# Four m tiles of x on GpSimd's queue, in transfers of 15 partitions

## The chip, the cores and the metric

The kernel runs on one core of a Trainium2 chip. The metric is the device time of one execution in microseconds (us). A profile of one execution gives, beside that time, the span of its instructions and what each engine did: PE (TensorE), PEld (its weight loads), DVE (VectorE), ACT (ScalarE), POOL (GpSimd) and SP (SyncE, which here only issues transfers). Sixteen DMA engines move the data between HBM and the on-chip memory.

## The reference

```python
batch, m, k, n = 16, 512, 1024, 768
# x: (batch, m, k), weight: (k, n), sub_value: (batch, m, n), all float32
return (np.matmul(x, weight) - sub_value).astype(np.float32)
```

One weight serves all batches, so this is a single product of (8192 x 1024) by (1024 x 768), less a matrix of the size of the output.

## The kernel before, in words

The 8192 rows are 64 m tiles of 128 rows. `SEGMENTS` puts them in eight groups of 8: partition p of a group holds 8 consecutive rows, so that a transfer of n tiles of a group moves, for each partition, one contiguous row of n x 4 KB of x, or n x 3 KB of `sub_value` or of the output. "x 56" below is the transfer of x that begins with tile 56; s stands for `sub_value` and o for the output.

For each tile: SP loads x into `x_ring` (16 tiles deep) and s into `so_ring` (32 tiles deep). ACT casts x to float16 (`cast`, L330). x is then transposed, for most tiles by TensorE as pairs of halves read as float32 words (L348), after which ACT copies the result from PSUM (L361); for the nine pairs named in `ON_DVE` by DVE in blocks of 32 (L381). TensorE multiplies the transposed tile with the float16 weight that stays on chip, 16 matmuls into one of three product buffers `po_b` (L200). DVE subtracts s from the product into `so_ring` (`finish`, L430), and SP stores the output from there. TensorE's order is written by hand: the transposes of tile t stand between the matmuls of tile t - 2. The cast of tile t is put on ACT at the matmuls of tile t - 4 (t - 7 for a pair in `ON_DVE`), ahead of the copies of later transposes. Each engine runs its instructions in order.

SP's transfers run in the order of the list `TRANSFERS`, and each waits on SP, with all later ones behind it, until its ring places are free: x for the casts of the tiles 16 before, s for the landing of the outputs 32 before, o for the subtractions. Entries of kind "p" are x as well, but `issue` puts them on GpSimd's own queue (L260 to L269), where they wait apart from SP. In the kernel before there is one, tile 63, split by `PARTS` into partitions 120 to 125, 0 to 120 and 125 to 128. It waits for the cast of tile 47, which had the place before, and for the landing of tile 62. The cast of tile 63 waits for the semaphores of all three parts.

Of the kernel before, what the change touches and what calls it, by code (L numbers as in the profile page):

```python
# [14 lines left out]
NX, NSO = 16, 32  # L15
# [14 lines left out]
    ('x', 0, 1), ('w', 0, 1), ('x', 1, 1), ('w', 1, 1), ('x', 2, 1), ('w', 2, 1),  # L30
    ('x', 3, 2), ('w', 3, 1), ('s', 0, 1), ('x', 5, 3), ('s', 1, 3), ('x', 8, 4),
    ('s', 4, 4), ('x', 12, 4), ('s', 8, 8), ('x', 16, 2), ('x', 18, 6), ('s', 16, 8),
    ('x', 24, 8), ('o', 0, 8), ('s', 24, 8), ('x', 32, 8), ('s', 32, 8), ('x', 40, 8),
    ('o', 8, 8), ('o', 16, 8), ('s', 40, 8), ('x', 48, 8), ('s', 48, 8), ('x', 56, 7), ('p', 63, 1),
    ('o', 24, 8), ('o', 32, 8), ('s', 56, 8), ('o', 40, 8), ('o', 48, 8), ('o', 56, 5),
    ('o', 61, 2), ('o', 63, 1),
]

PARTS = (120, 125), (0, 120), (125, 128)


class Queue:
# [65 lines left out]
def kernel(  # L108
# [7 lines left out]
    nc = tc.nc  # L116

    x_flat = x.flatten_outer_dims()
# [4 lines left out]
    _, N = weight.shape  # L123
# [6 lines left out]
    def view(flat, at, n):  # L130

        first, size = next(one for one in SEGMENTS if one[0] <= at < sum(one))
        assert at + n <= first + size
        rows = flat[first * P : (first + size) * P].rearrange("(p j) c -> p j c", p=P, j=size)
        return rows[:, at - first : at - first + n]
# [6 lines left out]
    def sbuf(name, shape, dtype):  # L142
        return ctx.enter_context(nc.sbuf_tensor(name, shape, dtype)).ap()
# [10 lines left out]
    x_ring = sbuf("x_ring", [P, NX, K], F32)  # L154
# [12 lines left out]
    counter = {}  # L167
# [4 lines left out]
    def count(name):  # L172
        so_far[name] += 1
        return (counter[name], 1)

    sp, pe = Queue(nc, nc.sync), Queue(nc, nc.tensor)
    act, dve, pool = Queue(nc, nc.scalar), Queue(nc, nc.vector), Queue(nc, nc.gpsimd)
# [6 lines left out]
        out=along, data0=ones, data1=ones, initial=0.0, op0=mybir.AluOpType.mult, op1=mybir.AluOpType.add,  # L184
    ), waits=[(counter["ident"], 1)], then=count("ident"))
    dve.add(lambda: nc.vector.transpose(across, along), waits=[(counter["ident"], 3)], then=count("ident"))
    for a in range(P // Q):
        here = slice(a * Q, (a + 1) * Q)
        dve.add(lambda here=here: nc.vector.tensor_tensor(  # L189
            out=ident[here, here], in0=along[here], in1=across[here], op=mybir.AluOpType.is_equal,  # L190
# [16 lines left out]
    landed = {}  # L207
    cast_at, evac_at, pair_at, turn_at, mul_at, finish_at, w_at = {}, {}, {}, {}, {}, {}, {}
# [22 lines left out]
    def lane(tag):  # L231

        for one in lanes:
            if one["tags"] <= known:
                break
        else:
            one = {"sem": tc.alloc_semaphore(f"lane{len(lanes)}"), "value": 0, "tags": set()}
            lanes.append(one)
        one["value"] += 16
        one["tags"].add(tag)  # L240
        return one["sem"], one["value"]

    def issue():
        nonlocal known
        while todo:
            kind, at, n = todo[0]
            span = set(range(at, at + n))
            old = {t - NX if kind == "x" else t - NSO for t in span}
            need, by = {
                "w": (set(), "o"),  # L250
                "x": ({t for t in old if t >= 0}, "cast"),
                "p": ({at - NX}, "cast"),
                "s": ({t for t in old if t >= 0}, "o"),
                "o": (span, "finish"),
            }[kind]
            if not need <= done[by]:
                return
            todo.pop(0)
            done["x" if kind == "p" else kind] |= span
            if kind == "p":  # L260
                here, there = x_ring[:, at % NX], view(x_flat, at, 1)[:, 0]
                waits, landed["x", at] = [(counter["cast"], cast_at[at - NX]), *landed["x", at - 1]], []
                for low, high in PARTS:
                    sem = tc.alloc_semaphore(f"part{low}")
                    pool.add(lambda low=low, high=high, here=here, there=there: nc.gpsimd.dma_start(  # L265
                        out=here[low:high], in_=there[low:high], max_dma_last_dim=2048,
                    ), waits, (sem, 16))
                    landed["x", at].append((sem, 16))
                continue  # L269
            if kind == "w":  # L270

                first = NSO - 2 * (n_c - at)
                st = so_ring[:, first : first + 2]
                sem, value = lane((kind, at))
                sp.add(lambda st=st, at=at: nc.sync.dma_start(out=st, in_=w_c[at]), then=(sem, 16))  # L275
                for r in range(2):
                    dve.add(
                        lambda at=at, r=r, st=st: nc.vector.tensor_copy(out=w_sb[:, at, r], in_=st[:, r]),  # L278
                        waits=[(sem, value)], then=count("w"),
                    )  # L280
                    staged[first + r] = so_far["w"]
                w_at[at] = so_far["w"]
                continue
            ring, size, flat = {
                "x": (x_ring, NX, x_flat), "s": (so_ring, NSO, sub_flat), "o": (so_ring, NSO, out_flat)
            }[kind]
            here = ring[:, at % size : at % size + n]
            there = view(flat, at, n)
            waits = []
            if kind == "x" and need:  # L290
                waits.append((counter["cast"], max(cast_at[t] for t in need)))
                last = max(need, key=lambda t: cast_at[t])
                known |= {tag for t, tag in of_x.items() if t in cast_at and cast_at[t] <= cast_at[last]}
            if kind == "s":
                for t in need:
                    waits += landed["o", t]
                    known.add(of_o[t])
                for t in span:
                    if t % NSO in staged:
                        waits.append((counter["w"], staged.pop(t % NSO)))  # L300
                        known |= {("w", c) for c in w_at if w_at[c] <= waits[-1][1]}
            if kind == "o":
                waits.append((counter["finish"], max(finish_at[t] for t in need)))
                known |= {of_s[t] for t in finish_at if finish_at[t] <= max(finish_at[u] for u in need)}
            sem, value = lane((kind, at))
            for t in span:
                landed[kind, t] = [(sem, value)]
                {"x": of_x, "s": of_s, "o": of_o}[kind][t] = (kind, at)
            if kind == "o":
                here, there = there, here  # L310
            sp.add(lambda here=here, there=there: nc.sync.dma_start(out=here, in_=there), waits, (sem, 16))  # L311

    def cast(mi):
        assert mi in done["x"]
        done["cast"].add(mi)
        x_in = x_ring[:, mi % NX]
        first = mi - mi % 2
        waits = list(landed["x", mi])
        if first in ON_DVE:
            if mi == first:  # L320
                b, before = take("x16p", N16P, mi)
                if before is not None:
                    waits.append((counter["pair"], pair_at[before]))
            to = x16p_b[:, slot["x16p", first], mi - first]
        else:
            b, before = take("x16", N16, mi)
            if before is not None:
                waits.append((counter["turn"], turn_at[before]))
            to = x16_b[:, b]
        act.add(lambda: nc.scalar.copy(out=to, in_=x_in), waits, count("cast"))  # L330
        cast_at[mi] = so_far["cast"]
        issue()
# [92 lines left out]
    def finish(mi):  # L425
        assert mi in done["s"]
        done["finish"].add(mi)
        o = so_ring[:, mi % NSO].rearrange("p (h n) -> p h n", h=2)
        po = po_b[:, slot["po", mi]]
        dve.add(lambda: nc.vector.tensor_tensor(  # L430
            out=o, in0=po[:, :, :NS], in1=o, op=mybir.AluOpType.subtract
        ), [*landed["s", mi], (counter["mul"], mul_at[mi])], count("finish"))
        finish_at[mi] = so_far["finish"]
        issue()

    issue()


# [59 lines left out]
    for mi in range(HEAD + (EARLY is not None), n_mt):  # L498
# [3 lines left out]
        t = mi + TA  # L502
# [68 lines left out]
```

## Time and profile before

| | |
|---|---|
| median of 2 runs | 210.94 us (210.79 to 211.09) |
| the profiled execution: its time, its span | 210.47 us, 208.6 us |
| PE busy | 195.2 us, 94% |
| DVE busy | 128.1 us, 61% |
| ACT busy | 109.0 us, 52% |
| POOL busy | 3.0 us, 1% |
| DMA | 87.08 MB, 417 GB/s over the span |
| last output's transfer, 384 KB | 4.8 us from issue to landing |

The time of an execution is its span and some 1.9 us around it. Busy times are those of one execution; "to landing" is counted from the issue of a transfer to its completion semaphore. The views of the profile are the page (busy times, 40 equal slices of the span, DMA queues, the chain that ended last, groups of instructions by line, DMA issues), the waits, the timeline, and windows of time. In the page, q1 is SP's queue and q0 GpSimd's.

### The profile page before, as it was taken

What the parts mean: (1) busy time and instruction counts of PE and PEld (TensorE: products, weight loads), DVE (VectorE), ACT (ScalarE), POOL (GpSimd) and SP (SyncE); (2) the same over time, 40 slices, a digit from 0 to 9 for tenths busy, and PEclk for the clock granted to TensorE, in tenths of its full rate; (3) what the DMA queues carried; (4) which work ended last, traced back from release to release, by engine and by line L of the source; (5) the groups of instructions that cost most, each with busy time, mean ns of one, the idle gap of its engine ahead of it and who ended that gap; (6) DMA issues with size and microseconds to landing.
All of it is one profiled execution on the core that took longest, in us unless ns stands there. A gap on an engine that the chain in (4) does not pass through costs nothing.

```text
span 208.6 us, 2617 instructions
## 1 busy us (share of the span) xinstructions
PE 195.2 (94%) x1234; PEld 75.4 (36%) x700; DVE 128.1 (61%) x224; ACT 109.0 (52%) x113; POOL 3.0 (1%) x10
## 2 busy tenths in 40 slices
PE   6899699969999999999999999999999999999960
PEld 0233244324434433443443443344344344344310
DVE  2233224975993895597399389469739938942330
ACT  2655659506573761854745676183574746516300
POOL 1000000000000000000000000000000300000000
PEclk9999999999999999999999999999999999999997
DMA  6999999999999999999999999999999999999993
GB/s 204 421 428 429 437 423 431 449 435 427 424 440 446 371 443 433 444 421 411 455 440 427 415 429 448 430 452 404 424 441 428 433 432 423 443 424 433 421 418 155
DMA packets 5685, 87.08 MB, mean 417 GB/s; under 512 B 689, under 2 KB 689, under 8 KB 2097
## 3 DMA queue, kind: packets, MB, share of 16 engines
q1 hardware_dynamic: 5472, 86.51, 97.3%
q0 software_dynamic: 208, 0.52, 0.6%
q14 instruction: 4, 0.02, 0.0%
q8 instruction: 1, 0.02, 0.0%
HBM read 61.87 MB, written 25.17 MB: 417 GB/s over the span
## 4 chain that ended last, share of the span: by engine, by line
PE 75%; DMA 13%; DVE 6%; SPq 3%; issue 1%; DVEq 0%
PE po_b L200 67%; DMA so_ring<-in_sub_value_dram 13%; PE pt_b L348 8%; DVE xtp_b L381 3%; DVE so_ring L430 2%; SPq L311 2%; SPq L275 1%; SPq L566 0%; DVEq L61 0%; SPq L140 0%
## 5 line engine op out<-in xcount | busy, mean ns | idle before, releaser
L200 PE MATMUL po_b<-w_sb,xt_b 128*128 128x384 f16 x704 | 126.0, 326 | 0.9 <-DVE w_sb L278 0.8
L430 DVE TENSOR_TENSOR so_ring<-po_b,so_ring 128x768 f32<-128x768 f32 x64 | 60.7, 957 | 58.9 <-PE po_b L200 39.8
L361 ACT COPY xt_b<-pt_b 128x1024 f16<-128x1024 f16 x44 | 44.5, 1012 | 64.7 <-PE pt_b L348 63.8
L381 DVE STREAM_TRANSPOSE xtp_b<-x16p_b 32x256 f32<-32x256 f32 x144 | 62.7, 435 | 2.3
L200 PE MATMUL po_b<-w_sb,xtp_b 128*128 128x384 f16 x320 | 61.3, 326 | 1.8 <-DVE xtp_b L381 1.7
L410 PEld LDWEIGHTS <-xt_b 128*128 128x128 f16 x352 | 34.4, 98 | 58.4 <-issue 55.2
L330 ACT CAST x_b<-x_ring 128x1024 f16<-128x1024 f32 x46 | 47.2, 1048 | 5.5 <-DMA x_ring<-in_x_dram 5.5
L348 PE MATMUL pt_b<-ident,x_b 128*128 128x128 f32 x184 | 47.6, 274 | 1.9 <-ACT x_b L330 1.9
L348 PEld LDWEIGHTS pt_b<-ident,x_b 128*128 128x128 f32 x184 | 25.3, 141 | 45.0 <-issue 36.3
L330 ACT CAST x16p_b<-x_ring 128x1024 f16<-128x1024 f32 x18 | 18.8, 1046 | 14.8 <-DMA x_ring<-in_x_dram 14.8
L410 PEld LDWEIGHTS <-xtp_b 128*128 128x128 f16 x160 | 15.7, 98 | 20.3 <-issue 18.3
L278 DVE CAST w_sb<-so_ring 128x768 f16<-128x768 f32 x8 | 4.1, 557 | 12.0 <-DMA so_ring<-in_weight_dram 12.0
L200 PE MATMUL po_b<-idle_x,idle_w 128*128 128x512 f16 x26 | 7.7, 443 | 1.7 <-POOL idle_x L180 1.7
L265 POOL DMA_DIRECT2D x_ring<-in_x_dram x3 | 2.0, 668 | 136.7 <-DMA x_ring<-in_x_dram 136.7
L361 ACT COPY xtp_b<-pt_b 128x1024 f16<-128x1024 f16 x2 | 2.0, 1012 | 2.4 <-PE pt_b L348 2.4
L330 ACT ACT_TABLE_LOAD x1 | 1.3, 1283 | 0.9 <-SPq L140 0.9
L440 PEld LDWEIGHTS <-idle_w 128*128 128x128 f16 x4 | 0.4, 100 | 1.7 <-POOL idle_x L180 1.7
L189 DVE TENSOR_TENSOR ident<-along,across 32x32 f32<-32x32 f32 x4 | 0.7, 183 | 0.1
L181 DVE MEMSET ones<- 128x32 f32 x1 | 0.1, 85 | 1.0 <-SPq L140 1.0
L180 POOL MEMSET idle_x<- 128x512 f16 x1 | 0.5, 531 | 0.0
L489 POOL MEMSET mark<- 128x1 f32 x1 | 0.1, 99 | 24.0 <-ACT xtp_b L361 24.0
L512 ACT CAST stub<-ident 128x1 f16<-128x1 f32 x2 | 0.4, 194 | 0.0
(8 smaller groups left out, 1.2 us busy)
## 6 DMA issues: line engine op xcount, KB each, us to landing
so_ring<-in_sub_value_dram SPq DMA_DIRECT2D x7, 3072.0 KB, 24.2
out_dram<-so_ring SPq DMA_DIRECT2D x7, 3072.0 KB, 26.6
x_ring<-in_x_dram SPq DMA_DIRECT2D x4, 4096.0 KB, 21.6
x_ring<-in_x_dram SPq DMA_DIRECT2D x2, 2048.0 KB, 27.2
x_ring<-in_x_dram SPq DMA_DIRECT2D x1, 3584.0 KB, 21.9
so_ring<-in_weight_dram SPq DMA_DIRECT2D x4, 768.0 KB, 8.8
x_ring<-in_x_dram SPq DMA_DIRECT2D x1, 3072.0 KB, 28.3
x_ring<-in_x_dram SPq DMA_DIRECT2D x2, 1024.0 KB, 24.8
```

What stands on the lines that cost most here:

```text
L189: dve.add(lambda here=here: nc.vector.tensor_tensor(out=ident[here, here], in0=along[here], in1=across[here], op=mybir.AluOpType.is_equal, ...
L200: return nc.tensor.add_instruction(mybir.InstMatmult(name=nc.get_next_instruction_name(), engine=full.engine, ins=list(full.ins), outs=lis ...
L265: pool.add(lambda low=low, high=high, here=here, there=there: nc.gpsimd.dma_start(out=here[low:high], in_=there[low:high], max_dma_last_di ...
L275: sp.add(lambda st=st, at=at: nc.sync.dma_start(out=st, in_=w_c[at]), then=(sem, 16))
L278: lambda at=at, r=r, st=st: nc.vector.tensor_copy(out=w_sb[:, at, r], in_=st[:, r]),
L311: sp.add(lambda here=here, there=there: nc.sync.dma_start(out=here, in_=there), waits, (sem, 16))
L330: act.add(lambda: nc.scalar.copy(out=to, in_=x_in), waits, count("cast"))
L348: pe.add(lambda: nc.tensor.transpose(words, from_, ident), waits, count("turn") if last else None)
L361: act.add(lambda: nc.scalar.copy(out=to, in_=pt_b[:, b]), waits, count("evac"))
L381: dve.add(lambda: nc.vector.transpose(xt[b * Q : (b + 1) * Q, :, a * Q : (a + 1) * Q], x16[a * Q : (a + 1) * Q, :, b * Q : (b + 1) * Q],), ...
L410: pe.add(lambda weights=weights: nc.tensor.ldweights(weights, tile_position=(0, 0)), [w for w in waits if w[0] in ready])
L430: dve.add(lambda: nc.vector.tensor_tensor(out=o, in0=po[:, :, :NS], in1=o, op=mybir.AluOpType.subtract), [*landed["s", mi], (counter["mul" ...
```

## The change

Tiles 38, 39 and 62 leave SP's queue: the transfer x 32 has 6 tiles instead of 8, and x 56 has 6 instead of 7. They and tile 63 are loaded by GpSimd as two groups of two tiles. Each tile of a group goes in eight transfers of 15 partitions, first the eight of the one tile, then those of the other, and at the end one transfer of the last 8 partitions for each: 18 transfers to a group, each with a semaphore of its own. The group of tile 38 waits for the casts of tiles 22 and 23 alone; that of tile 62 for the casts of tiles 46 and 47 and for the landing of tile 61. Each of the four casts waits for the nine semaphores of its tile. No other instruction changes its place on any engine.

```diff
-    ('x', 24, 8), ('o', 0, 8), ('s', 24, 8), ('x', 32, 8), ('s', 32, 8), ('x', 40, 8),
-    ('o', 8, 8), ('o', 16, 8), ('s', 40, 8), ('x', 48, 8), ('s', 48, 8), ('x', 56, 7), ('p', 63, 1),
+    ('x', 24, 8), ('o', 0, 8), ('s', 24, 8), ('x', 32, 6), ('p', 38, 2), ('s', 32, 8), ('x', 40, 8),
+    ('o', 8, 8), ('o', 16, 8), ('s', 40, 8), ('x', 48, 8), ('s', 48, 8), ('x', 56, 6), ('p', 62, 2),
...
-PARTS = (120, 125), (0, 120), (125, 128)
+PARTS = [(j, low, low + 15) for j in range(2) for low in range(0, 120, 15)] + [(j, 120, 128) for j in range(2)]
...
             if kind == "p":
-                here, there = x_ring[:, at % NX], view(x_flat, at, 1)[:, 0]
-                waits, landed["x", at] = [(counter["cast"], cast_at[at - NX]), *landed["x", at - 1]], []
-                for low, high in PARTS:
-                    sem = tc.alloc_semaphore(f"part{low}")
-                    pool.add(lambda low=low, high=high, here=here, there=there: nc.gpsimd.dma_start(
-                        out=here[low:high], in_=there[low:high], max_dma_last_dim=2048,
+                here, there = x_ring[:, at % NX : at % NX + n], view(x_flat, at, n)
+                waits = [(counter["cast"], max(cast_at[t] for t in old))]
+                if at > NSO + 8:
+                    waits += landed["x", at - 1]
+                for t in span:
+                    landed["x", t] = []
+                for k, (j, low, high) in enumerate(PARTS):
+                    sem = tc.alloc_semaphore(f"part{at}_{k}")
+                    pool.add(lambda j=j, low=low, high=high, here=here, there=there: nc.gpsimd.dma_start(
+                        out=here[low:high, j], in_=there[low:high, j], max_dma_last_dim=2048,
                     ), waits, (sem, 16))
-                    landed["x", at].append((sem, 16))
+                    landed["x", at + j].append((sem, 16))
                 continue
```

## The prediction

> **What bounds the kernel now.** I read the page from the top: the busy table, the 40 slices, the DMA queues, then the chain, the waits, and the timeline of the last 50 us. The slices come first.
>
> ```profile
> PE   6899699969999999999999999999999999999960
> ...
> POOL 1000000000000000000000000000000300000000
> ...
> DMA  6999999999999999999999999999999999999993
> ...
> q1 hardware_dynamic: 5472, 86.51, 97.3%
> q0 software_dynamic: 208, 0.52, 0.6%
> ```
>
> TensorE and the 16 DMA engines are both full from the fourth slice or so to the end: two bounds side by side, so a delay in either is paid unless the other's buffers cover it. POOL shows one mark, in slice 32: the three transfers of tile 63. The line of q0 carries most of this forecast. Those three transfers have only 128 partition rows of 4 KB (0.52 MB), yet 208 packets, which is 16 x 13. The trace's records of single packets say what the 13 of each engine are: one packet per partition row, or an 8 byte stand-in on an engine that a transfer leaves out, and one 4 byte completion packet per transfer. Most engines have 2 + 9 + 2 packets for the three transfers (8 rows, or stand-ins, and a completion in the middle one).
>
> The DMA groups give the landing of these transfers, the timeline their issue and what consumes x at the end:
>
> ```profile
> x_ring<-in_x_dram POOLq DMA_DIRECT2D x1, 480.0 KB, 14.7
> ...
> x_ring<-in_x_dram POOLq DMA_DIRECT2D x1, 20.0 KB, 6.8
> x_ring<-in_x_dram POOLq DMA_DIRECT2D x1, 12.0 KB, 15.8
> ```
> ```profile
> 162.45 2.00 POOL L265 DMA_DIRECT2D x_ring<-in_x_dram  x3 [136.72 <-DMA x_ring<-in_x_dram]
> ```
> ```profile
> 187.26 1.01 ACT L361 COPY xt_b<-pt_b 128x1024 f16<-128x1024 f16 x1 [5.24 <-PE pt_b L348]
> 188.17 1.05 ACT L330 CAST x_b<-x_ring 128x1024 f16<-128x1024 f32 x1
> 189.12 0.19 ACT L512 CAST stub<-ident 128x1 f16<-128x1 f32 x1
> 190.29 1.01 ACT L361 COPY xt_b<-pt_b 128x1024 f16<-128x1024 f16 x1 [0.98 <-PE pt_b L348]
> 191.20 1.05 ACT L330 CAST x_b<-x_ring 128x1024 f16<-128x1024 f32 x1
> ```
> ```profile
> 190.69 0.27 PE L348 MATMUL pt_b<-ident,x_b 128*128 128x128 f32 x1
> ```
>
> A 12 KB transfer took 15.8 us: not its bytes cost, but its place in line. The two casts are tiles 62 and 63. The cast of 62 ends at 189.2 and TensorE's first transpose of tile 62 starts at 190.69, so 62 may be about 1.4 us late, that is, land by 189.5, before TensorE stops. Behind it on TensorE stand three transposes of 62, the rest of tile 60, and tiles 61 to 63. Nothing there can pass.
>
> **The turn of a software packet.** On every engine the packet records show strict alternation while both queues have work: one q0 packet, one q1 packet. A 24 KB row of q1 takes 0.91 us, a 4 KB row of q0 0.16, a stand-in or completion 0.01; one in nine q1 packets is itself a completion. So a q0 packet of any size waits 0.91 x 8/9 = 0.81 us on average. Tile 63: 12 waits of 0.81 and 8 rows of 0.16 make 11.0 us; the records span 167.2 to 177.7 on a typical engine, 10.5.
>
> [...]
>
> **The change, part by part.** Removed: the three transfers of tile 63, and from SP's queue tiles 38 and 39 (x 32 has 6 tiles instead of 8) and tile 62 (x 56 has 6 instead of 7). Added: two groups of 18 transfers on GpSimd. Each engine gets 16 rows per group, spread evenly, but also, per transfer, a completion, and a stand-in where it is left out. 16 transfers x 2 packets + 2 x 2 = 36 packets per engine and group, 20 of them carrying no data. Over both groups q0 should have 2 x 36 x 16 = 1152 packets.
>
> *Issue.* 18 x 0.668 us = 12 us per group on POOL, which has nothing else to do. It is hidden as long as one transfer takes under 2 turns, 1.8 us.
>
> *Tiles 38 and 39.* The wait is the cast of tile 23, which ends at 68.7 (timeline), no landing. First packets 4.6 us after the first issue, as at tile 63 (162.45 to 167.06): 73.4. 36 packets x 0.81 + 16 x 0.16 = 31.9, slightly more where rows are 32 KB (1.21 us): done by 107. Tile 38 is cast at 118.8. Margin over 10 us; cost nothing. SP's loads around it carry 2.4 us less and share with 2.5 us more: all later landings move by +0.3 us. The nearest deadline of those, s of tile 56 (landing 185.1, needed some 0.6 us later before TensorE misses a product buffer), holds, because x 56 is shorter by 8 x 0.15 = 1.2 us per engine and q0's rows beside it are about as many as before. One engine writes its output rows 3% slower than the others (0.945 against 0.912) and is the one that tile 63's 120 partitions left out; the even spread gives it 6 rows back, 0.9 us, which s 56 bears from that 1.2. From below: rows of x that leave SP's queue could bring s 56 1 us earlier; it is waited for by DVE alone, so no gain. I take 0.
>
> *Tiles 62 and 63.* x 56 lands at 161.85 - 1.2 + 0.3 = 161.0; issue at 161.6, first packets at 166.2. SP's queue has rows for all that time (outputs 32, s 56, outputs 40 and 48, 32 rows per engine). Tile 62 is complete with packet 34 (its last 8 partitions are the 17th transfer): 34 x 0.81 + 15 x 0.16 = 29.9, so 196.1; on the slow engine 24 output rows x 0.03 = 0.7 more: 196.8. Tile 63 comes with packet 36, 1.8 us later, in time for its own cast behind that of 62. The cast of 62 runs 196.8 to 197.9 instead of 188.17 to 189.22. TensorE, due at 190.69, goes on at 197.9: **stall 7.2 us**. ACT's copy of tile 61 waits behind this cast too, but is needed after it.
>
> *Clock.* 7.2 us idle is longer than the 4.4 us after which this trace shows the clock at 0.5. Coming back costs half of the ramp. The kernel's first matmuls start at 1.68 and the full clock is on record from 4.5: half of 2.8 is **1.4 us**. [...]
>
> *Tail.* Before, the last output was issued at about 202.5 and landed 4.8 us later, behind rows still queued. Delayed by 8.6 us it finds the queue nearly empty (outputs 48 end near 199): start of data after about 1.8 us, 1.0 us of rows (384 KB), 0.6 of spread, 3.4. **Gain 1.4 us**; bounds 0.8 and 2.
>
> *Waits.* Each of the four casts waits for 9 semaphores instead of 1 or 3; all but the last are long up. Under 0.5 us on ACT, hidden at 38 and 39, inside the rounding at 62.
>
> Sum: 7.2 + 1.4 - 1.4 = +7.2 us. The profiled execution took 210.47 (span 208.6 plus 1.9); 217.7 in that execution's terms. The median of the runs is 210.94, 0.47 above it: 218.1, and I say **218.0**.
>
> **Rivals.** (A) is the above, own range 214 to 222.5: landing 194.5 to 200.5 by how the turns fall, with or without the clock.
>
> (B) Not slower. Completions and stand-ins of many small transfers might be taken together with the row beside them, so that a transfer costs one turn: 18 turns x 0.81 + 2.5 = 17.1, tile 62 complete near 183, before 188.17. The point is 189.5: up to there nothing is lost. Then only packet overhead and the slow engine's 6 rows remain: 210.9 + 0.3 = 211.2. For it: when SP's queue gives only a completion in its turn, two q0 packets follow closely. Against: at tile 63 a completion sat behind a full 24 KB row on nearly every engine.
>
> (C) GpSimd becomes the limit. If one issue took 2.5 us instead of 0.67 (many transfers in flight, rings to refill), a group takes 45 us: tile 62 near 161.6 + 17 x 2.5 + 4 = 208, a stall of 18 us, and tile 38 at about 115, still in time: 210.9 + 18 + 1.4 - 1.4 = 229. Against: the three issues before took 572 to 754 ns.
>
> **How the numbers follow.** A 0.83, B 0.13, C 0.04. This measurement tells about 2% (4.2 us) from no change. Slower by more: A but for its lowest end, and C, 0.84; within: B and that end, 0.14; faster 0.02, within B, if even loading brings the last outputs forward further than I see. Range 212 to 223: A's with the upper part of B.
>
> **What would show it.** Right: q0 with 1152 packets; POOL busy twice for about 12 us, near 69 and 162; a new wait of ACT on x near 188 to 197, and of PE on ACT's cast, together most of the loss, with none near 119; granted clock 0.5 for a few us after; the last output landing in under 4 us. Wrong: x of tile 62 landing before 189 (then B), a stall near 119 or 187, or POOL busy far over 12 us per group (C).

## The result and the profile after

The changed kernel takes 227.55 us (median of 2 runs, 226.62 to 228.48) against 210.94: 1.079 times the time before, 95% interval 1.060 to 1.098. The forecast was slower, 218.0 with a range of 212 to 223. The direction was foreseen, and less than half of the loss: 7.1 of 16.6 us.

The page of the changed kernel, slices and DMA queues:

```profile
PE   7997899799999999989998999996999999703990
...
POOL 1000000000006910000000000000029500000000
PEclk9999999999999999999999999999999999975899
DMA  6999999999999999999999999999999999995372
GB/s 214 424 422 435 445 423 442 415 450 433 446 430 377 447 383 327 357 335 349 375 443 418 424 433 442 446 407 437 437 433 417 431 374 371 429 431 230 131 314 115
...
q1 hardware_dynamic: 5472, 84.94, 91.8%
q0 software_dynamic: 1152, 2.10, 2.6%
```

A slice is 5.62 us. The hole in PE near 200 us and the dip of the clock behind it are the ones that were forecast, and 1152 packets on q0 is the count that was forecast. What was not is in the row GB/s. In slices 16 to 20, 84 to 112 us, the DMA engines move 327 to 375 GB/s instead of some 430, while the row above it says that they are busy all the time. Slices 33 and 34 have it again. Busy engines that move less: their packets take longer.

The dip was forecast from these windows of the kernel before, where TensorE's work ends near 201.5 and half clock stands from 206 (third column from the end: the granted clock):

```profile
200.00:204.00 4.00, 1.48 (x10) 0.29 (x3) 0.96 (x1) 0.00 (x0) 0.00 (x0) 1.00 0.95 402
204.00:205.80 1.80, 0.00 (x0) 0.00 (x0) 0.00 (x0) 0.00 (x0) 0.00 (x0) 1.00 0.70 287
206.00:208.60 2.60, 0.00 (x0) 0.00 (x0) 0.00 (x0) 0.00 (x0) 0.00 (x0) 0.50 0.06 24
```

The timelines of the changed kernel, of GpSimd's transfers, of ACT's casts of tiles 62 and 63, and of TensorE's four transposes of tile 62 and the first of tile 63:

```profile
69.16 10.18 POOL L269 DMA_DIRECT2D x_ring<-in_x_dram  x18 [43.61 <-ACT x16p_b L334]
167.43 10.04 POOL L269 DMA_DIRECT2D x_ring<-in_x_dram  x18 [88.09 <-DMA x_ring<-in_x_dram]
```
```profile
204.75 1.04 ACT L334 CAST x_b<-x_ring 128x1024 f16<-128x1024 f32 x1 [11.81 <-DMA x_ring<-in_x_dram]
...
206.70 1.04 ACT L334 CAST x_b<-x_ring 128x1024 f16<-128x1024 f32 x1
```
```profile
205.85 0.47 PE L352 MATMUL pt_b<-ident,x_b 128*128 128x128 f32 x1 [8.75 <-ACT x_b L334]
...
207.39 0.42 PE L352 MATMUL pt_b<-ident,x_b 128*128 128x128 f32 x1
...
208.88 0.42 PE L352 MATMUL pt_b<-ident,x_b 128*128 128x128 f32 x1
...
210.27 0.27 PE L352 MATMUL pt_b<-ident,x_b 128*128 128x128 f32 x1
...
211.03 0.27 PE L352 MATMUL pt_b<-ident,x_b 128*128 128x128 f32 x1
```

The cast of tile 62 starts at 204.75 instead of 188.17, and TensorE stands for 8.75 us in front of the first transpose. The next ones are 1.5 us apart at first, at half clock, and 0.76 once the clock is back. But GpSimd's second group already starts 5 us later than before (167.43 against 162.45), so something was lost earlier.

TensorE runs the same 1234 matmuls in the same order in both kernels, so I subtracted the start of each from that of the same matmul before. The delay grows in a few steps:

| start before, us | delay after the step, us | what came late |
|---|---|---|
| up to 97 | 0.1 | |
| 97.2 | 1.3 | s of tile 24 |
| 120.7 to 121.4 | 2.8 | x 40 |
| 149.3 | 4.7 | s of tile 40 |
| 187.0 | 6.3 | s of tile 56 |
| 190.7 | 15.2 | x of tile 62 |
| to 192.8 | 17.3 | half clock |

For the first four steps the right column follows from the waits. The first fence is the kernel before, the second the changed one: DVE's subtractions of tiles 24, 40 and 56 and ACT's cast of tile 40.

```profile
89.60 0.96 DVE L430 TENSOR_TENSOR so_ring<-po_b,so_ring 128x768 f32<-128x768 f32 x1
...
136.85 0.96 DVE L430 TENSOR_TENSOR so_ring<-po_b,so_ring 128x768 f32<-128x768 f32 x1 [3.77 <-DMA so_ring<-in_sub_value_dram]
...
185.47 2.69 DVE L430 TENSOR_TENSOR so_ring<-po_b,so_ring 128x768 f32<-128x768 f32 x3 [2.67 <-DMA so_ring<-in_sub_value_dram]
...
115.01 1.05 ACT L330 CAST x16p_b<-x_ring 128x1024 f16<-128x1024 f32 x1 [2.48 <-DMA x_ring<-in_x_dram]
```
```profile
91.79 0.96 DVE L434 TENSOR_TENSOR so_ring<-po_b,so_ring 128x768 f32<-128x768 f32 x1 [2.08 <-DMA so_ring<-in_sub_value_dram]
...
142.82 1.82 DVE L434 TENSOR_TENSOR so_ring<-po_b,so_ring 128x768 f32<-128x768 f32 x2 [6.88 <-DMA so_ring<-in_sub_value_dram]
...
192.24 2.69 DVE L434 TENSOR_TENSOR so_ring<-po_b,so_ring 128x768 f32<-128x768 f32 x3 [4.76 <-DMA so_ring<-in_sub_value_dram]
...
121.05 1.05 ACT L334 CAST x16p_b<-x_ring 128x1024 f16<-128x1024 f32 x1 [7.26 <-DMA x_ring<-in_x_dram]
```

And TensorE's own waits in the changed kernel, at the first matmuls of tiles 28, 36, 46 and 59:

```profile
98.49 0.81 PE L200 MATMUL po_b<-w_sb,xtp_b 128*128 128x384 f16 x4 [0.97 <-DVE xtp_b L385]
...
123.14 0.81 PE L200 MATMUL po_b<-w_sb,xt_b 128*128 128x384 f16 x4 [1.06 <-ACT xt_b L365]
...
153.94 0.81 PE L200 MATMUL po_b<-w_sb,xtp_b 128*128 128x384 f16 x4 [1.72 <-DVE xtp_b L385]
...
193.25 0.81 PE L200 MATMUL po_b<-w_sb,xtp_b 128*128 128x384 f16 x4 [1.42 <-DVE so_ring L434]
```

The way from a late transfer to TensorE is indirect. DVE waits for s of tile 24, and the block transposes of tiles 28 and 29 stand behind that subtraction on DVE; s of tile 40 holds up those of tiles 46 and 47 in the same way. On ACT the cast of tile 40 waits for x 40, and the copy that TensorE needs for tile 36 stands behind it. s of tile 56 keeps the product buffers full. x 32 and x 48 came late too, but others ended the waits.

The span ends 16.2 us later (224.8 against 208.6). So 6.3 us are gone before tile 62 is even due. The forecast had nothing there.

The records of single packets say where. Of SP's 24 KB rows, those of outputs (stored rows) still take 0.92 us while GpSimd's packets stand between them (74 to 80 us); those of loads (loaded rows) take 1.14 us on average from 85 to 107 us, with a median of 1.20. Summed over the early group, loaded rows took 5.5 us per engine more than rows of their length take elsewhere (0.91 us for 24 KB, 1.06 for 28 KB, 1.21 for 32 KB). This is called the excess below.

### The profile page after: what moved, and what is told of

Read it like the earlier page. It is cut to its first block, busy times and chain, and to the rows that moved or that the text cites. A ratio compares the mean times of both kernels' runs of the same rounds, so it can differ in the third digit from the quotient of the medians.

```text
span 224.8 us, 2665 instructions
## 1 busy us (share of the span) xinstructions
PE 198.8 (88%) x1234; PEld 75.9 (34%) x700; DVE 127.9 (57%) x224; ACT 108.5 (48%) x113; POOL 21.2 (9%) x43
## 3 DMA queue, kind: packets, MB, share of 16 engines
q0 software_dynamic: 1152, 2.10, 2.6%
## 4 chain that ended last, share of the span: by engine, by line
DMA 60%; PE 24%; POOL 4%; ACT 4%; DVE 3%; issue 2%; SPq 1%; ACTq 0%; DVEq 0%
DMA x_ring<-in_x_dram 44%; PE po_b L200 21%; DMA so_ring<-in_sub_value_dram 16%; POOL x_ring L269 4%; PE pt_b L352 3%; ACT x_b L334 2%; DVE xtp_b L385 2%; ACT xt_b L365 1%; DVE so_ring L434 1%; SPq L315 1%; SPq L279 0%; ACTq L61 0%; SPq L61 0%; ACT x16p_b L334 0%; SPq L570 0%
## 5 line engine op out<-in xcount | busy, mean ns | idle before, releaser
L200 PE MATMUL po_b<-w_sb,xt_b 128*128 128x384 f16 x704 | 128.1, 329 | 1.9 <-ACT xt_b L365 1.1
L352 PE MATMUL pt_b<-ident,x_b 128*128 128x128 f32 x184 | 48.1, 276 | 10.4 <-ACT x_b L334 10.3
L269 POOL DMA_DIRECT2D x_ring<-in_x_dram x36 | 20.2, 564 | 131.7 <-DMA x_ring<-in_x_dram 88.1
```

The lines of the kernel that those rows point to most:

```text
L200: return nc.tensor.add_instruction(mybir.InstMatmult(name=nc.get_next_instruction_name(), engine=full.engine, ins=list(full.ins), outs=lis ...
L269: pool.add(lambda j=j, low=low, high=high, here=here, there=there: nc.gpsimd.dma_start(out=here[low:high, j], in_=there[low:high, j], max_ ...
L352: pe.add(lambda: nc.tensor.transpose(words, from_, ident), waits, count("turn") if last else None)
```

## The experiments

### Which group costs what

Tiles 62 and 63 alone in the new form; then tiles 38 and 39 alone. Diffs are against the changed kernel unless said otherwise, and "..." stands for lines left out.

```diff
-    ('x', 24, 8), ('o', 0, 8), ('s', 24, 8), ('x', 32, 6), ('p', 38, 2), ('s', 32, 8), ('x', 40, 8),
+    ('x', 24, 8), ('o', 0, 8), ('s', 24, 8), ('x', 32, 8), ('s', 32, 8), ('x', 40, 8),
```

> Tiles 62 and 63 go as in the changed kernel (18 transfers on GpSimd's queue), tiles 38 and 39 stay on SP's queue (x 32 with 8 tiles). Both theories on the slow load rows agree here; this run splits the loss by group. The forecast had all of the loss in this group: 218, with x of tile 62 cast at 196.8. From the changed kernel's trace, where from the first software packet to the cast of 62 some 33 us pass instead of the 30 of the forecast, and s of tile 56 is late as well: cast of 62 near 199 to 200, a stall of TensorE of about 9 to 10 us, the clock's return 2 us, a tail 1 us shorter: 220 to 222, and no delay of TensorE before 185 us.

Measured: 219.34 us, ratio 1.041 (1.039 to 1.043), a little under what was expected.

```diff
-    ('o', 8, 8), ('o', 16, 8), ('s', 40, 8), ('x', 48, 8), ('s', 48, 8), ('x', 56, 6), ('p', 62, 2),
+    ('o', 8, 8), ('o', 16, 8), ('s', 40, 8), ('x', 48, 8), ('s', 48, 8), ('x', 56, 7), ('p', 63, 1),
...
+PARTS_OF = {63: [(0, 120, 125), (0, 0, 120), (0, 125, 128)]}
...
-                for k, (j, low, high) in enumerate(PARTS):
+                for k, (j, low, high) in enumerate(PARTS_OF.get(at, PARTS)):
```

> Tiles 38 and 39 go as in the changed kernel, tiles 62 and 63 as in the kernel before (x 56 with 7 tiles, tile 63 in its three transfers). The forecast: +0.3 us, 211. From the changed kernel's trace: rows that SP's queue loads (24 KB) take 1.15 us on average instead of 0.91 while GpSimd's packets stand between them, stored rows stay at 0.91; x 40 and x 48 land late and TensorE is some 4.7 us behind at 150 us; nothing gives that back: 215 to 216.5.

Measured: 217.94 us, ratio 1.035 (1.032 to 1.039), above what was expected. The two losses, 8.6 and 7.2 us, come to 15.8 of the 16.6 of the whole change. The late group alone behaves nearly as forecast: TensorE has no delay until 187 us, then waits for the cast of tile 62, which starts at

```profile
198.76 1.04 ACT L334 CAST x_b<-x_ring 128x1024 f16<-128x1024 f32 x1 [10.90 <-DMA x_ring<-in_x_dram]
```

(ACT's timeline, late group alone) where the forecast had 196.8. The early group alone, which was put at 0.3 us, leaves TensorE 4.3 us behind at 149 us and 5.8 at 187; its excess is 5.6 us per engine. The rest of its 7.2 us lies behind TensorE's end and comes up again at the tail below.

### Completions, or rows?

The first guess came from the same packet records: a loaded row that was followed by one of GpSimd's completions was longer (1.24 us) than one followed by a data row (about 1.0). Two kernels have the same bytes under the same waits with fewer transfers.

```diff
-PARTS = [(j, low, low + 15) for j in range(2) for low in range(0, 120, 15)] + [(j, 120, 128) for j in range(2)]
+PARTS = [(j, 0, 128) for j in range(2)]
```

> Tiles 38, 39, 62 and 63 on GpSimd's queue under the same waits, but each in one transfer of 128 partitions: the same bytes, 2 transfers per group instead of 18. Completion theory (a loaded row of SP's queue that is followed by a completion of GpSimd's queue is held up by about 0.33 us, by a data row only 0.07): 18 packets per engine and group instead of 36, 2 completions: rows near 0.98, some 1.5 us of DMA time lost beside the loads in the early group, no stall on tile 62 (9 packets, complete near 176): 211 to 213. Data theory (any loaded row of GpSimd's queue beside a loaded row of SP's holds it up by about 0.25 us): 16 rows per engine still cost 4 us in the early group: 214 to 216, rows near 1.15.

Measured: 211.09 us, ratio 1.0018 (1.0011 to 1.0026). All of the loss is gone but 0.33 us.

```diff
+PARTS = [(j, low, low + 60) for j in range(2) for low in (0, 60)] + [(j, 120, 128) for j in range(2)]
```

> As the changed kernel, but with transfers of 60 partitions instead of 15 (4 rows per engine): 6 transfers per group, 28 packets at most per engine instead of 36. Completion theory: 6 x 0.33 + 16 x 0.07 = 3 us of DMA time lost beside loads in the early group, tile 62 complete near 188 to 190, a stall of 0 to 2 us: 212.5 to 215. Data theory: as with whole tiles 4 us and the stall: 215 to 217. In both, between whole tiles and transfers of 15.

Measured: 216.49 us, ratio 1.027 (1.025 to 1.029).

Transfers of 60 have an excess of 3.1 us per engine, just the 3 that the completion theory asked for, though the time lies above its range and within that of the data theory. Whole tiles speak against both. Their packets stand beside loads as well (129 of their data rows between 82 and 91 us, and completions), and the excess is 0.02 us, not 1.5. That refutes the data theory outright, and the completion theory too unless its cost depends on something else. With transfers of 60, moreover, it is the rows between two data rows that are slow (0.23 us over on average, from 80 to 101 us), with no completion next to them. What is left as a candidate is not what a packet is but which partitions its transfer takes, and with them perhaps which engine carries them.

### The same rows in two orders

Two kernels move tile 39 alone on GpSimd's queue, in 16 transfers of 8 partitions with a step of 4, in pairs of one from the lower half of the partitions (0, 4 .. 28) and one from the upper half (64, 68 .. 92); tile 63 goes as in the kernel before. They differ only in the order within each pair. That the order changes which engine carries which row was the author's guess; the records do not number the engines. First the lower half before the upper:

```diff
...
+PARTS = [(0, half + low, half + low + 29) for low in (0, 1, 2, 3, 32, 33, 34, 35) for half in (0, 64)]
...
+                        out=here[low:high:step, j], in_=there[low:high:step, j], max_dma_last_dim=2048,
...
```

> Only tile 39 leaves SP's queue (x 32 with 7 tiles), in 16 transfers of 8 partitions with a step of 4: 0, 4 .. 28 and 64, 68 .. 92 in turn, then the same from 1, 2, 3, 32, 33, 34 and 35; tile 63 goes as in the kernel before. Each engine gets 8 rows, 8 stand-ins and 16 completions, as many completions as in the early group of the changed kernel. [...] Completion theory: 16 x 0.33 = 5 us of lost DMA time beside loads, 214 to 216. Source theory (15 reads at once that lie 32 KB apart in HBM): no excess or more of it, the reads lie 128 KB apart here: 211 to 216.

Measured: 211.86 us, ratio 1.0053 (1.0033 to 1.0074), excess 0.04 us per engine. TensorE ends 0.16 us later than before; the rest of the 1.1 us lies behind its end (see the tail below).

The other order, against the run with the lower half first:

```diff
-PARTS = [(0, half + low, half + low + 29) for low in (0, 1, 2, 3, 32, 33, 34, 35) for half in (0, 64)]
+PARTS = [(0, half + low, half + low + 29) for low in (0, 1, 2, 3, 32, 33, 34, 35) for half in (64, 0)]
```

> [...]

Measured: 214.18 us, ratio 1.0205 (1.0141 to 1.0269), excess 2.5 us per engine. Its four runs, 213.8 to 216.7 us, all lie above the four with the lower half first, 211.4 to 212.1.

Windows of both, the run with the lower half first ahead: start and end, length, busy time of PE, PEld, DVE, ACT and POOL with instructions, granted clock, DMA share, GB/s.

```profile
88.00:95.00 7.00, 7.00 (x47) 2.80 (x26) 6.79 (x14) 3.90 (x5) 0.00 (x0) 1.00 0.99 425
95.00:102.00 7.00, 7.00 (x47) 2.70 (x25) 4.02 (x6) 2.71 (x4) 0.00 (x0) 1.00 0.97 414
```
```profile
88.00:95.00 7.00, 7.00 (x47) 2.77 (x26) 6.42 (x13) 3.90 (x5) 0.00 (x0) 1.00 1.03 399
95.00:102.00 7.00, 7.00 (x47) 2.75 (x26) 4.28 (x7) 2.69 (x4) 0.00 (x0) 1.00 1.00 371
```

The same number of transfers, packets, completions and bytes, the same engine shares (0.97 to 1.03), and 371 GB/s instead of 414 with nothing but the order changed. Loaded 24 KB rows take 0.912 us with the lower half first, 1.013 with the upper half first. The lower half first has 16 completions per engine, nearly as many as the changed kernel's group, and none of its excess: the completion theory falls here. In the reversed pair a loaded row behind a stand-in is as long as one behind a row of data (1.08 and 1.06 us on average, from 80 to 105 us; 0.95 behind a completion). So an engine is held up also where it carries no data of GpSimd's queue itself. That fits a row of another engine as the cause; no run shows which.

Two more runs, with the early group alone, test the rest. First, the source in HBM; the kernel then loads other rows of x for tiles 38 and 39, so its output is not the product and only its time counts:

```diff
...
-                        out=here[low:high, j], in_=there[low:high, j], max_dma_last_dim=2048,
+                        out=here[low:high, j], in_=x_flat[P * (at + j) + low : P * (at + j) + high] if at == 38 else there[low:high, j], max_dma_last_dim=2048,
...
```

> The early group of the changed kernel alone (tiles 62 and 63 as before), but its 15 rows come from 15 neighbouring rows of x in HBM, 60 KB in one piece, and not from rows 32 KB apart: the data of tiles 38 and 39 is other rows of x, all else is the same. Source theory: the excess of loaded rows goes (rows at 0.91, 211.2). [...]

Measured: 218.3 us, ratio 1.036 (1.034 to 1.037), excess 6.5 us per engine. That the rows lie 32 KB apart in HBM is not the cause. If the reversed pair changes which engine carries a row, it changes which one reads it from HBM as well as which one writes it, and no run separates the two; that rows from another place in HBM lose as much speaks for the side that is written.

Second, 16 partitions to a transfer:

```diff
...
+PARTS = [(j, low, low + 16) for j in range(2) for low in range(0, 128, 16)]
...
```

> The early group alone, in 16 transfers of 16 neighbouring partitions: 16 engines each, so no engine is left out and there are no stand-ins; 16 rows and 16 completions per engine, 32 packets. [...] Completion theory: 16 completions for 18, 216 to 218. If the stand-ins or the rotation of the left-out engine were the cause: 211.5.

Measured: 217.98 us, ratio 1.034 (1.032 to 1.036), excess 5.8 us per engine. In its profile the clock fell for 3.4 us as well, so the excess is the better measure here. Without stand-ins and without a left-out engine it is about that of the early group (5.6), so rotating the left-out engine is not what costs. The windows of transfers of 16 show 311 GB/s where whole tiles, below them, have 446:

```profile
88.00:95.00 7.00, 7.00 (x47) 2.66 (x25) 3.92 (x8) 3.91 (x4) 0.00 (x0) 1.00 0.94 311
```
```profile
88.00:95.00 7.00, 7.00 (x47) 2.70 (x25) 5.38 (x13) 3.90 (x5) 0.00 (x0) 1.00 1.04 446
```

### The turns of the late group, with little excess

The lower half first also allows a test of the step that was forecast: many packets, and little excess (0.5 us per engine, most of it in one burst near 180 us, against 1.4 in the late group alone). The late group alone, in 2 x 16 transfers of 8 partitions, each tile in 32 packets per engine (1024 packets on q0).

```diff
...
+PARTS = [(j, half + low, half + low + 29) for j in range(2) for low in (0, 1, 2, 3, 32, 33, 34, 35) for half in (0, 64)]
...
```

> [...] Turn theory (one packet of GpSimd's queue per packet of SP's): from a first packet near 165.9, 31 waits of 0.81 and 8 rows of 0.16 make 26.4, 0.7 more on the engine that stores slowly: tile 62 is complete at 193 and TensorE stops for 3 to 4 us in front of it; tile 63 would need until 219, but SP's queue runs thin near 199 and lets the rest through, 202 to 205: a second stop of 6 to 9 us. With the clock 220 to 224, slower than with the transfers of 15 in the late group alone, although s of tile 56 is in time and rows stay at 0.91. [...]

Measured: 220.13 us, ratio 1.047 (1.042 to 1.052). ACT's timeline:

```profile
194.23 1.04 ACT L334 CAST x_b<-x_ring 128x1024 f16<-128x1024 f32 x1 [6.15 <-DMA x_ring<-in_x_dram]
...
202.60 1.04 ACT L334 CAST x_b<-x_ring 128x1024 f16<-128x1024 f32 x1 [6.32 <-DMA x_ring<-in_x_dram]
```

Tile 62 comes after 32 packets, about 1 us later than expected, and tile 63 after 64, within what was expected. TensorE stops twice, for 4.7 and 3.6 us; 6 to 9 were expected for the second stop. The return of the clock follows the first. Counting packets gives the landing where SP's rows are hardly held up. That it is slower than transfers of 15 in the late group alone is not certain: the intervals overlap.

## Why the prediction was wrong, point by point

- **Tiles 38 and 39: the step that failed.** It said: "Margin over 10 us; cost nothing", and for SP's loads "all later landings move by +0.3 us". The two tiles were indeed in time (last packet at 112.1 us; the sum in the prediction gives 105.1, since 36 x 0.81 + 16 x 0.16 is 31.7 and not 31.9). But the step priced GpSimd's rows by their own length, 16 x 0.16 us, and left SP's rows at 0.91 us. Measured, SP's loaded rows took 1.14 us while GpSimd's packets stood between them (85 to 107 us): 5.5 us per engine in the group. s of tile 24, x 40 and s of tiles 40 and 56 came late one after the other, and TensorE was 6.3 us behind at 187. The DMA engines have no idle time in which to make that up (the row DMA stands at 9 tenths from the second slice to the 36th). The prediction called s of tile 56 the nearest deadline; s of tile 24 was missed 90 us earlier. Stalls near 119 and 187 were among its signs of being wrong, and both came.
- **Why it was not seen:** the only transfers of GpSimd in the trace before, tile 63's, stood mostly beside stored rows, which are not held up (0.92 us in the changed kernel, 74 to 80 us). The trace could not show the price, and the forecast carried over a zero without bounding it from above.
- **Packets and turns: right.** 1152 packets on q0, 36 per engine and group, one turn each. With hardly any excess the count gave 193 for tile 62, measured 194.2; in the late group alone it gave 196.8, measured 198.8, of which the excess of its loaded rows explains 1.35 us and 0.6 stays open.
- **Issue: right.** 18 transfers took 10.2 us on POOL (558 ns each; 668 were taken) and delayed nothing until the end of the kernel; rival C is refuted.
- **Tiles 62 and 63: right place, short in size.** The stall was put at 7.2 us. TensorE's delay grows by 9.2 us with the late group alone. In the changed kernel it grows by 8.9, and that this is close to 7.2 is luck: tile 62 came 8.0 us later than forecast, because its group started 5.7 us later (first packet 171.9 instead of 166.2) and SP's rows met the excess again, but TensorE was 6.3 us late itself.
- **The margin of s of tile 56:** it was said to hold. In the late group alone it holds (0.0 us of delay at 187); in the changed kernel it adds 1.6 us.
- **Clock: right in kind, 2.1 us instead of 1.4.** The record of the granted clock shows half clock from 199.91 to 210.15, that is, 4.3 us beyond the restart at 205.85, where 2.8 us was taken. That the clock comes back after a stop as it rose at the kernel's start (1.68 to 4.5) was the author's estimate; no run shows it, and 4.3 us, half of it lost, were measured in its place. One fall and one rise were too few to forecast from, as the last section shows.
- **Tail: the sum right by luck.** 1.4 us was taken, and 17.3 of delay became 16.2 of span, 1.1. But the last output landed 2.3 us after its issue instead of 4.8, a gain of 2.5, and 1.4 of it was lost behind the landing: the records show GpSimd's drain instruction at the end, for which the other engines wait, at 3.00 us instead of 0.31. The prediction had no such term. The drain is also some 0.7 of the 1.1 us that the run with the lower half first loses.
- **Rival B** (a turn per transfer, 211) is refuted by tile 62's landing: it put it near 183, and it came near 198.8 with the late group alone. The 0.3 us that it left for packet overhead and for loading the slow engine evenly agrees with whole tiles, +0.33 us, though that run does not separate the two.

Put together: 7.2 + 1.4 - 1.4 was forecast; 6.3 (loads held up, with 0.1 from the start) + 8.9 + 2.1 - 1.1 = 16.2 was measured.

## What to carry to other kernels

When DMA engines are full, a transfer on a second queue must be priced by what it does to the rows beside it, and not by its own bytes: loads through GpSimd's queue left SP's rows at 0.91 us in transfers of 128 partitions and in those of 8 with a step of 4, the lower half first, and cost SP's loads 1.2 to 2.6 times their own length in transfers of 15, 16 and 60 partitions and with the upper half first. Why is not shown, so another shape or order has to be measured. Count packets, completions and stand-ins included: beside a full queue each took a turn behind a row of the other queue here (the count of turns put tile 62 at 193 and 196.8 us, where its cast began at 194.2 and 198.8), so many small transfers landed late however few bytes they had; and each transfer added some 0.08 us to GpSimd's drain at the end. When a full queue is slowed, look at every load that follows, s as well as x, and at the engine that works through it in order: the first deadline to be missed here was not the one that had been named. And when the trace before shows an operation only beside stores, it says nothing of its price beside loads; bound that from above.

## What the runs showed of the hardware that was not expected

- Loaded rows of SP's queue take up to 1.20 us (median, 24 KB) instead of 0.91 while rows of 4 KB go in transfers of 15 partitions. Stored rows in the same place stay at 0.92 (74 to 80 us) and 0.91 (193 to 203 us). The order of the same transfers alone makes 0.912 or 1.013 us, as the reversed pair shows; that it acts through which engine writes which partitions is the author's guess, and no run looks into that.
- A row of GpSimd's queue can cost the loads more than its own length. With the upper half first the excess is 2.5 us per engine for 8 rows, 0.31 for each row of 0.16 us, although some of these rows stood beside stores. GpSimd's rows themselves stay near their length (changed kernel: 0.16 us in the median, 0.17 on average). Why the loads lose more than 0.16 stays open.
- A row's follower only seemed to matter: with the lower half first rows before a completion and rows before data both take 0.91 us. In the changed kernel most rows before a completion stand behind a row of data (141 of 165, from 80 to 107 us). With transfers of 60, where the two can be told apart, rows behind data take 1.15 us whichever follows, and rows behind a completion 0.95 to 0.98.
- GpSimd's drain at the end of the program grows with the number of its transfers: 0.31 us with 3, 0.40 with 4, 1.53 with 18, 2.68 with 32 and 3.00 with 36, some 0.08 us for each. Packets do not count: 4 transfers and 18, both with 576 packets, took 0.40 and 1.53.
- The granted clock does not follow from the length of a stop alone. In the five kernels where it fell before the end, half clock lasted 10.24 us (changed kernel, late group alone) or 3.41 (transfers of 60, transfers of 16, late group in transfers of 8), three times 3.41 or once. A stop of TensorE of 1.95 us, ended at 124.5, brought it with transfers of 16 (from 125.7), and one of 3.6 us did not (the second stop of the late group in transfers of 8).
